# A depthwise convolution moved from VectorE, ScalarE and GpSimd to TensorE, with rows moved between partitions by DMA

## The chip, the cores and the metric

One core of one Trainium2 chip. The metric is the device time of one launch in microseconds (us), the median of the runs. The engines are PE (TensorE: matmuls, with PEld its weight loads), DVE (VectorE), ACT (ScalarE), POOL (GpSimd) and SP (SyncE, which here issues every DMA).

## What is computed

One block of a hybrid network over 512 tokens of 1024 channels, plus 256 context tokens, in float32: a modulated RMS norm, then two mixers on the same input (a Conformer convolution and a latent attention with 8 heads), merged by gates and one projection, then a SwiGLU feed-forward part and a final norm. The part that matters here is the convolution:

```python
def conformer_conv(conv_in, w_dw, b_dw, ln_g, ln_b, w_pw):
    a, g = jnp.split(conv_in, 2, axis=-1)
    u = a * jax.nn.sigmoid(g)
    u = lax.conv_general_dilated(
        u, w_dw[:, None, :], window_strides=(1,),
        padding=((CONV_WIDTH // 2, CONV_WIDTH // 2),),
        dimension_numbers=('NWC', 'WIO', 'NWC'),
        feature_group_count=D_CONV) + b_dw
    u = jax.nn.silu(layer_norm(u, ln_g, ln_b))
    return u @ w_pw
```

It is depthwise: every one of the 1024 channels has 31 taps of its own along the tokens. The layer norm behind it needs all channels, so nothing of the convolution is read before all eight of its tiles are done.

## The kernel before, in words

Activations lie transposed: a tile has 128 channels as partitions and the 512 tokens as columns. Every product of the block is made of three matmuls (`mm3`, L137 to L139): an operand is split into a high part that TensorE's float32r takes whole and the low rest (`split`, the high part by ACT at L104, the low by DVE at L105; for weights `split_w`, ACT L121 and DVE L125), and hi x hi, hi x lo and lo x hi are summed in PSUM. Weights come from HBM as tiles `wr` by SP (`load_w`).

After a prologue whose order is written out by hand (to about 140 us) comes the attention, where a scheduler orders each engine by a priority that grows along the program. The loop over the heads h runs, in this order: two quarters of `scores(h, qb)` (10 matmuls each at L468 and L469 into one of two PSUM buffers `ps_s`, then the maximum on DVE, the exponential and the scaling on ACT); half of `conv_steps(h + 2)`; the other two quarters; the rest of `conv_steps`; `prep(h + 1)`, which makes the next head's queries and keys; gates in heads 6 and 7 (`gate_mla`); and `attend(h)`: for each of six blocks of keys four transposes of the probabilities (L486), a split into `ph` and `pl`, and three matmuls with the values.

`conv_steps(i)` makes tile i of the convolution's input, `u`: 48 matmuls at L319, and the gate product at L333, in a tile with 15 columns of zeros at each side. `conv_taps(i, u)` is the depthwise convolution of this tile, 31 taps. For the tiles of `DVE_TILES`, 1, 4 and 7, all 31 taps are a chain on DVE (L344, L346), each adding a shifted copy of `u` times one weight per partition to an accumulator in PSUM. For the other five ACT scales the shifted copy (L351) and POOL adds it (L352). The taps are put in with a priority 3000 later than their place (`later(TAPS_LATER)`), so that other work goes first where it is ready. All engines run their instructions in order, once the scheduler has laid them down.

After the attention come the remaining gates, the layer norm of the convolution's tiles, the projections, and the feed-forward part, with PE as the engine that is hardly ever idle.

Of the kernel before, what the change touches and what calls it, by code (L numbers as in the profile page):

```python
# [18 lines left out]
P = 128  # L19
D = 1024  # L20
KD = D // P
S = 512
C = 256
H = 8
TAPS = 31
PAD = TAPS // 2
FF = 2816
KF = FF // P
EPS = 1e-6
TAPS_LATER = 3000  # L30
# [13 lines left out]
WK_AT = (1, 4)  # L44
MODS = (3, 3, 3)
MCOLS = (2, 4, 7)
DVE_TILES = (1, 4, 7)
PE_KC = (2, 2, 2, 2, 2, 2, 2, 2)
WARM = (34, 9, 3)
SCALE = (128 + 64) ** -0.5  # L50
# [1 line left out]
VEC = {}  # L52
_off = 0
for _n, _w in (("c", 8), ("cc", 8), ("b_mod", 48), ("g_mix", 8), ("g_ffn", 8), ("g_q", 3), ("g_kv", 2),
               ("b_dw", 8), ("ln_g", 8), ("ln_b", 8), ("g_final", 8), ("w_dw", 8 * TAPS)):
    VEC[_n] = (_off, _off + _w)
    _off += _w
NVEC = _off
# [3 lines left out]
def block_kernel(ctx: ExitStack, tc: tile.TileContext, I, out):  # L62
# [2 lines left out]

    cp = ctx.enter_context(tc.tile_pool(name="cp", bufs=1))
    wp = ctx.enter_context(tc.tile_pool(name="wp", bufs=3))
    ap = ctx.enter_context(tc.tile_pool(name="ap", bufs=60))
    tp = ctx.enter_context(tc.tile_pool(name="tp", bufs=3))
    sm = ctx.enter_context(tc.tile_pool(name="sm", bufs=4))  # L70
    bp = ctx.enter_context(tc.tile_pool(name="bp", bufs=4))
# [92 lines left out]
    bm1 = cp.tile([P, 16], F32, name="bm1")  # L164
    dve.tensor_scalar(out=bm1[:, 0:8], in0=v("b_mod", 8, 8), scalar1=1.0, scalar2=None, op0=ALU.add)
    dve.tensor_scalar(out=bm1[:, 8:16], in0=v("b_mod", 32, 8), scalar1=1.0, scalar2=None, op0=ALU.add)
    wdw = cp.tile([P, KD * TAPS], F32, name="wdw")
    dve.tensor_scalar(out=wdw, in0=v("w_dw"), scalar1=0.5, scalar2=None, op0=ALU.mult)
    modc = cp.tile([P, 32], F32, name="modc")

    def rstd_cols(ps, n, nb):
# [21 lines left out]
    def ps_x(n=512):  # L193
        return pp.tile([P, 512], F32, tag="x", name=nm("px"), bufs=4)[:, 0:n]
# [125 lines left out]
                yield  # L320

    def conv_steps(i, wg=None, wa=None):
        u = bp.tile([P, S + 2 * PAD], F32, tag="u", name=nm("u"), bufs=4)
        yield u
        ps = ps_x()
        yield from mm_steps(ps, wg or wtile(I["w_in"][3 + KD + i]), hx)
        sg = temp()
        act.activation(sg, ps, AF.Tanh, scale=0.5)
        ps = ps_x()
        yield from mm_steps(ps, wa or wtile(I["w_in"][3 + i]), hx)  # L330
        pool.memset(u[:, 0:PAD], 0.0)
        pool.memset(u[:, PAD + S:], 0.0)
        dve.scalar_tensor_tensor(out=u[:, PAD:PAD + S], in0=sg, scalar=1.0, in1=ps, op0=ALU.add, op1=ALU.mult)  # L333

    def conv_taps(i, u):
        a = slot()
        conv[i] = a
        acc = ps_x() if i in DVE_TILES else a
        for j in range(TAPS):
            wcol = wdw[:, i * TAPS + j:i * TAPS + j + 1]  # L340
            src = u[:, j:j + S]
            if i in DVE_TILES:
                if j == 0:
                    dve.tensor_scalar(out=acc, in0=src, scalar1=wcol, scalar2=v("b_dw", i), op0=ALU.mult, op1=ALU.add)  # L344
                else:
                    dve.scalar_tensor_tensor(out=a if j == TAPS - 1 else acc, in0=src, scalar=wcol, in1=acc, op0=ALU.mult, op1=ALU.add)  # L346
            elif j == 0:
                act.activation(a, src, AF.Identity, scale=wcol, bias=v("b_dw", i))
            else:
                t = bp.tile([P, S], F32, tag="tap", name=nm("tap"), bufs=3)  # L350
                act.activation(t, src, AF.Copy, scale=wcol)  # L351
                pool.tensor_tensor(out=a, in0=a, in1=t, op=ALU.add)  # L352

    def evac(ps, n=512):
        h, l = slot(F32R), slot(F32R)
# [121 lines left out]
        act.activation(p, p, AF.Copy, scale=r)  # L477
        return p

    def attend(h, ps_):  # L480
        g, e = h // 2, h % 2
        po = ps_x()
        for kb in range(6):
            pt = ps_x()
            for qb in range(4):
                pe.transpose(pt[:, qb * P:(qb + 1) * P], ps_[qb][:, kb * P:(kb + 1) * P], ident)  # L486
            ph, pl = pair()
            split(pt, ph, pl)
            vh, vl = vt[g][kb // 2]
            o = (kb % 2) * 256 + e * P  # L490
            mm3(po, vh[:, o:o + P], vl[:, o:o + P], ph, pl, kb == 0, kb == 5)
        a = slot()
        act.copy(a, po)
        o_t[h] = a

    def gate_w(i, after=None):
        raw = wp.tile([P, D], F32, tag="wr", name=nm("wr"))
# [19 lines left out]
    with tc.manual_schedule(engines={ET.PE, ET.DVE, ET.Activation, ET.Pool, ET.SP}):  # L517
# [230 lines left out]
        stack_q(1, terms)  # L748
        prep_kc(*wu, 768, 0, kx)
        prep_v(*wv, 0)  # L750
    with later(TAPS_LATER):
        conv_taps(0, u0)
        conv_taps(1, u1)

    for h in range(H):
        pr = [scores(h, qb) for qb in range(2)]
        if h < 6:
            it = conv_steps(h + 2)
            u = next(it)
            pump(it, 24)  # L760
        pr += [scores(h, qb) for qb in range(2, 4)]
        if h < 6:
            pump(it, 99)
            with later(TAPS_LATER):
                conv_taps(h + 2, u)
        if h + 1 < H:
            prep(h + 1)
        if h == 6:
            gate_mla(0, o_t[4])
        if h == 7:  # L770
            gate_mla(1, o_t[5])
            gate_mla(2, o_t[5])
        attend(h, pr)
    for i in range(3, KD):
        gate_mla(i, o_t[6])

# [1 line left out]
    if True:  # L778
# [73 lines left out]
                    dve.tensor_tensor(out=ssqs[q], in0=ssqs[q], in1=sq, op=ALU.add)  # L852

        for i in range(KD):
            t = slot() if i < 5 else bp.tile([P, S + 2 * PAD], F32, tag="u", name=nm("x2"), bufs=4)[:, 0:S]
            act.copy(t[:, 0:1], m1[0][:, 0:1])
            sp.dma_start(out=t, in_=I["xT"][:, i, :])
            x2.append(t)
# [310 lines left out]
```

## Time and profile before

| | |
|---|---|
| median of 3 runs | 1100.34 us (1097.81 to 1101.49) |
| the profiled execution | 1095.09 us |
| its span in the profile | 1093.3 us |
| mean granted clock of TensorE in it | 0.945 |
| PE busy | 972.0 us (89%) |
| DVE busy | 640.0 us (59%) |
| ACT busy | 525.4 us (48%) |
| POOL busy | 283.8 us (26%) |

Times are in us from the start of the span unless marked ns. An engine is busy while an instruction runs on it; register, branch, semaphore and DMA-issuing instructions don't count. [...] A name such as `px<-ph,stackr` means that the instruction writes `px` and reads `ph` and `stackr`; "idle before" is the time that the engine stood still just before an instruction, and the releaser is the instruction whose end it waited for. Matmuls are pipelined, so the time of one is longer than the step from one start to the next.

### The profile page before, as it was taken

To read this page: it belongs to the slowest core of one execution; us is meant where nothing else is said; L and a number is where in the kernel's file an instruction comes from. 1 tells how busy PE (TensorE), PEld (TensorE's weight loads), DVE (VectorE), ACT (ScalarE), POOL (GpSimd) and SP (SyncE) were. 2 spreads that over 40 slices of the span, in tenths; PEclk is the share of its full clock that TensorE was granted. 3 is DMA by queue.
4 is the path that set the end of the run, shared out by engine and by line. 5 is a ranking of instruction groups with operands and counts; after the bars stand their busy time and mean duration, and the time that the engine had idled before them with its cause. 6 is when DMAs were issued, how large, how long until landed. Compare 5 with 4: busy or idle time off the path is not lost.

```text
span 1093.3 us, 13176 instructions
## 1 busy us (share of the span) xinstructions
PE 972.0 (89%) x4772; PEld 812.0 (74%) x4772; DVE 640.0 (59%) x1052; ACT 525.4 (48%) x963; POOL 283.8 (26%) x237
## 2 busy tenths in 40 slices
PE   8789990988199962999999999999999999999996
PEld 8677880766187752777887888988888888888886
DVE  6997894465846568443589686483653333333333
ACT  4566686888168971554437223353333323332222
POOL 3766168998109991000000000020000000000000
PEclk9889995989599995999999999999999999999998
DMA  9801320011011000123363865133542223333312
GB/s 340 295 20 47 97 74 28 13 58 29 19 32 39 22 20 0 39 95 98 97 211 121 262 205 198 63 99 99 178 133 100 98 86 96 92 95 98 106 54 78
DMA packets 40721, 107.54 MB, mean 98 GB/s; under 512 B 4432, under 2 KB 6736, under 8 KB 40656
## 3 DMA queue, kind: packets, MB, share of 16 engines
q1 hardware_dynamic: 40656, 106.70, 30.3%
q8 instruction: 37, 0.61, 0.2%
q14 instruction: 28, 0.23, 0.1%
HBM read 104.59 MB, written 2.10 MB: 98 GB/s over the span
## 4 chain that ended last, share of the span: by engine, by line
PE 65%; DVE 13%; POOL 8%; ACT 8%; issue 5%; DMA 0%; POOLq 0%; SPq 0%; DVEq 0%; ACTq 0%
PE px L137 12%; PE px L138 11%; PE px L139 11%; POOL a L352 8%; PE ps L138 7%; PE ps L139 7%; PE ps L137 7%; DVE px L346 4%; DVE gm L263 2%; ACT tap L351 2%; PE ps L468 2%; DVE wl L125 2%; ACT p L477 1%; PE px L319 1%; ACT p L474 1%
## 5 line engine op out<-in xcount | busy, mean ns | idle before, releaser
L125 DVE TENSOR_TENSOR wl<-wr,wh 128x512 fp32r<-128x512 f32 (+1 forms) x264 | 197.2, 755 | 238.7 <-ACT wh L121 235.9
L121 ACT CAST wh<-wr 128x512 fp32r<-128x512 f32 (+2 forms) x274 | 164.5, 608 | 295.0 <-PE px L138 141.8
L137 PE MATMUL px<-a,wh 128*128 128x512 f32 (+1 forms) x607 | 224.2, 371 | 1.6 <-DVE t L417 1.0
L352 POOL TENSOR_TENSOR a<-a,tap 128x512 f32<-128x512 f32 x150 | 202.1, 1348 | 86.3 <-ACT tap L351 58.9
L138 PE MATMUL px<-a,wh 128*128 128x512 f32 (+1 forms) x607 | 223.1, 368 | 1.2 <-DVE a L722 1.1
L139 PE MATMUL px<-a,wl 128*128 128x512 f32 (+1 forms) x607 | 222.7, 367 | 0.0
L175 POOL TENSOR_TENSOR s<-s,mhalf 128x2 f32<-128x2 f32 (+1 forms) x10 | 9.3, 932 | 687.5 <-DVE s L173 687.5
L138 PE MATMUL ps<-a,wh 128*128 128x512 f32 (+1 forms) x376 | 141.6, 376 | 0.9 <-DVE a L921 0.8
L137 PE MATMUL ps<-a,wh 128*128 128x512 f32 (+1 forms) x376 | 141.5, 376 | 0.0
L139 PE MATMUL ps<-a,wl 128*128 128x512 f32 (+1 forms) x376 | 141.2, 375 | 0.0
L137 PEld LDWEIGHTS px<-a,wh 128*128 128x128 f32 x607 | 114.3, 188 | 22.1 <-ACT a L104 1.5
L138 PEld LDWEIGHTS px<-a,wh 128*128 128x128 f32 x607 | 114.4, 188 | 21.7 <-DVE a L722 2.0
L139 PEld LDWEIGHTS px<-a,wl 128*128 128x128 f32 x607 | 114.3, 188 | 18.9
L351 ACT ACTIVATE tap<-u,wdw 128x512 f32<-128x512 f32 x150 | 105.1, 722 | 33.8 <-POOL a L352 30.0
L138 PEld LDWEIGHTS ps<-a,wh 128*128 128x128 f32 x376 | 70.7, 188 | 14.3 <-DVE a L921 1.5
L319 PE MATMUL px<-a,wh 128*128 128x512 f32 x256 | 80.7, 393 | 0.0
L139 PEld LDWEIGHTS ps<-a,wl 128*128 128x128 f32 x376 | 70.8, 188 | 12.8
L137 PEld LDWEIGHTS ps<-a,wh 128*128 128x128 f32 x376 | 70.8, 188 | 12.6
L468 PE MATMUL ps<-a,a 128*128 128x512 f32 x160 | 60.1, 411 | 12.8 <-ACT a L104 12.8
L486 PE MATMUL px<-cst,p 128*128 128x128 f32 x192 | 30.7, 288 | 42.6 <-DVE a L346 42.2
L346 DVE SCALAR_TENSOR_TENSOR px<-u,wdw,px 128x512 f32<-128x512 f32 x87 | 65.6, 754 | 2.7
L486 PEld LDWEIGHTS px<-cst,p 128*128 128x128 f32 x192 | 25.2, 150 | 47.6 <-DVE a L346 42.6
(196 smaller groups left out, 1436.2 us busy)
## 6 DMA issues: line engine op xcount, KB each, us to landing
wr<-in_w_dram SPq DMA_DIRECT2D x60, 512.0 KB, 3.5
wr<-in_w_in_dram SPq DMA_DIRECT2D x35, 512.0 KB, 3.6
p<-in_w_mod_dram SPq DMA_DIRECT2D x64, 256.0 KB, 4.1
a<-in_w_mod_dram SPq DMA_DIRECT2D x32, 256.0 KB, 5.7
wr<-in_w_o_dram SPq DMA_DIRECT2D x8, 512.0 KB, 5.2
wr<-in_w_pw_dram SPq DMA_DIRECT2D x8, 512.0 KB, 5.6
wr<-in_w_out_dram SPq DMA_DIRECT2D x8, 512.0 KB, 3.7
a<-in_xT_dram SPq DMA_DIRECT2D x13, 256.0 KB, 5.6
```

Of the source, the lines that this page charges most:

```text
L121: act.copy(h, raw[:, i * WB:i * WB + h.shape[-1]])
L125: (eng or dve).tensor_tensor(out=l, in0=raw[:, i * WB:i * WB + h.shape[-1]], in1=h.bitcast(F32), op=ALU.subtract)
L137: pe.matmul(ps, lhsT=wh, rhs=ah, start=first, stop=False)
L138: pe.matmul(ps, lhsT=wh, rhs=al, start=False, stop=False)
L139: pe.matmul(ps, lhsT=wl, rhs=ah, start=False, stop=last)
L263: dve.scalar_tensor_tensor(out=gm[k], in0=slab(k, kc), scalar=sc[:, kc:kc + 1], in1=gm[k], op0=ALU.mult, op1=ALU.add)
L319: pe.matmul(ps, lhsT=l, rhs=r, start=k == 0 and i == 0, stop=k == n - 1 and i == 2)
L346: dve.scalar_tensor_tensor(out=a if j == TAPS - 1 else acc, in0=src, scalar=wcol, in1=acc, op0=ALU.mult, op1=ALU.add)
L351: act.activation(t, src, AF.Copy, scale=wcol)
L352: pool.tensor_tensor(out=a, in0=a, in1=t, op=ALU.add)
L468: pe.matmul(s[:, 0:512], lhsT=l[:, q0:q0 + P], rhs=rx_, start=i == 0, stop=i == 4)
L486: pe.transpose(pt[:, qb * P:(qb + 1) * P], ps_[qb][:, kb * P:(kb + 1) * P], ident)
```

## The change

The taps leave DVE, ACT and POOL. For a group of 32 channels, `tap_rows` has SP move the 32 rows of `u` (now its high and its low part side by side) four times from one place of SBUF to another, into the four quarters of the partitions of a tile `ur`, each copy 8 columns further on. A column of `ur` then holds 32 channels at four shifts. `tap_group` multiplies it by block matrices (`w_dwx`, 512 KB for a tile of 128 channels, made on the host): with `m` choosing one of two further shifts of 4 and the four quarters of the output `j` being shifts of 0 to 3, 4 x 2 x 4 = 32 taps, the last of them zero. That is two halves of 258 columns, each with two times three matmuls. ACT copies the sum to `e`, and SP moves each quarter of `e`, shifted by its `j`, to the rows of the 32 channels in one of four tiles `parts`. `tap_sum` adds the four on DVE. The moves of shifted rows stand in the program at the beginning of a head, the groups in `attend` after key blocks 1 to 4, the sum after the scores of the next head. The factor 0.5 of the gate goes from the weights to the copy `e`.

```diff
-    ap = ctx.enter_context(tc.tile_pool(name="ap", bufs=60))
+    ap = ctx.enter_context(tc.tile_pool(name="ap", bufs=58))
...
-    wdw = cp.tile([P, KD * TAPS], F32, name="wdw")
-    dve.tensor_scalar(out=wdw, in0=v("w_dw"), scalar1=0.5, scalar2=None, op0=ALU.mult)
...
     def conv_steps(i, wg=None, wa=None):
-        u = bp.tile([P, S + 2 * PAD], F32, tag="u", name=nm("u"), bufs=4)
+        u = bp.tile([P, 2, UPAD], F32R, tag="u", name=nm("u"), bufs=2)
...
-        dve.scalar_tensor_tensor(out=u[:, PAD:PAD + S], in0=sg, scalar=1.0, in1=ps, op0=ALU.add, op1=ALU.mult)
-
-    def conv_taps(i, u):
-        a = slot()
...
+        dve.scalar_tensor_tensor(out=sg, in0=sg, scalar=1.0, in1=ps, op0=ALU.add, op1=ALU.mult)
+        split(sg, u[:, 0, PAD:PAD + S], u[:, 1, PAD:PAD + S])
+
+    def tap_rows(u, g):
+        ur = bp.tile([P, 2, UW], F32R, tag="ur", name=nm("ur"), bufs=4)
+        for s_ in range(4):
+            sp.dma_start(out=ur[32 * s_:32 * s_ + 32].bitcast(F32), in_=u[32 * g:32 * g + 32, :, 8 * s_:8 * s_ + UW].bitcast(F32))
+        return ur
+
+    def tap_group(w, ur, g, parts):
+        ps = ps_s()
+        for q in range(2):
+            dst = ps[:, q * 512:q * 512 + HW]
+            for m in range(2):
+                o = (2 * g + m) * P
+                x = 4 * m + HW * q
+                mm3(dst, wc(w[0], o), wc(w[1], o), ur[:, 0, x:x + HW], ur[:, 1, x:x + HW], m == 0, m == 1)
+        e = bp.tile([P, 2 * HW], F32, tag="e", name=nm("e"), bufs=3)
+        act.activation(e.rearrange("p (q n) -> p q n", q=2), ps.rearrange("p (q n) -> p q n", q=2)[:, :, 0:HW], AF.Copy, scale=0.5)
+        for j in range(4):
+            sp.dma_start(out=parts[j][32 * g:32 * g + 32, :], in_=e[32 * j:32 * j + 32, j:j + S])
+
+    def tap_sum(i, parts):
+        a = parts[0]
         conv[i] = a
...
+        dve.scalar_tensor_tensor(out=a, in0=parts[1], scalar=v("b_dw", i), in1=a, op0=ALU.add, op1=ALU.add)
+        for t in parts[2:]:
+            dve.tensor_tensor(out=a, in0=a, in1=t, op=ALU.add)
...
-    def attend(h, ps_):
+    def attend(h, ps_, urs):
         g, e = h // 2, h % 2
         po = ps_x()
+        w = wtile(I["w_dwx"][h])
+        parts = [slot() for _ in range(4)]
...
+            if 1 <= kb <= 4:
+                tap_group(w, urs[kb - 1], kb - 1, parts)
...
+        return parts
...
-    with later(TAPS_LATER):
-        conv_taps(0, u0)
-        conv_taps(1, u1)
-
+    us = [u0, u1]
+    parts = None
     for h in range(H):
+        urs = [tap_rows(us[h], g) for g in range(4)]
         pr = [scores(h, qb) for qb in range(2)]
         if h < 6:
             it = conv_steps(h + 2)
-            u = next(it)
+            us.append(next(it))
             pump(it, 24)
         pr += [scores(h, qb) for qb in range(2, 4)]
         if h < 6:
             pump(it, 99)
-            with later(TAPS_LATER):
-                conv_taps(h + 2, u)
+        if parts:
+            tap_sum(h - 1, parts)
         if h + 1 < H:
             prep(h + 1)
...
-        attend(h, pr)
+        parts = attend(h, pr, urs)
+    tap_sum(7, parts)
```

What the scheduler makes of it on three engines, each row one instruction or several alike (the number behind a name is the buffer's):

DVE, before, around the taps of tile 4 (`u_2388` is that tile, `px_2503` the accumulator in PSUM, `a_2556` a part of head 3's query, which PE takes next):

```order
L333 SCALAR_TENSOR_TENSOR u_2388<-t_2462,px_2464 128x512
L125 TENSOR_TENSOR wl_2775<-wr_2770,wh_2773 128x512
L344 TENSOR_SCALAR px_2503<-u_2388,wdw,vec 128x512
L346 SCALAR_TENSOR_TENSOR px_2503<-u_2388,wdw,px_2503 128x512 x5
L125 TENSOR_TENSOR wl_2903<-wr_2899,wh_2901 128x512
L125 TENSOR_TENSOR wl_2904<-wr_2899,wh_2902 128x512
L346 SCALAR_TENSOR_TENSOR px_2503<-u_2388,wdw,px_2503 128x512 x24
L346 SCALAR_TENSOR_TENSOR a_2502<-u_2388,wdw,px_2503 128x512
L101 SCALAR_TENSOR_TENSOR a_2556<-px_2545,a_2555 128x512
```

All 31 taps of the tile stand ahead of the query's split; with the change these rows L344 and L346 are gone from DVE.

PE, now, in `attend(0)` (`px_1681` takes the transposes of a key block, `px_1623` gathers the head's output, `ps_1693` is the second group of taps):

```order
L495 MATMUL px_1681<-cst,p_1530 128x128
L138 MATMUL ps_1693<-ur_1409,wh_1626 128x258
L139 MATMUL ps_1693<-ur_1409,wh_1626 128x258
L140 MATMUL ps_1693<-ur_1409,wl_1628 128x258
L138 MATMUL ps_1693<-ur_1409,wh_1626 128x258
L139 MATMUL ps_1693<-ur_1409,wh_1626 128x258
L140 MATMUL ps_1693<-ur_1409,wl_1628 128x258
L138 MATMUL px_1623<-ph_1686,a_1382 128x512
L138 MATMUL ps_1693<-ur_1409,wh_1626 128x258
```

Before, the product of a key block stood right behind transposes; now tap matmuls are laid between the two.

DVE, now, at the scores of head 4 (`a_2985` to `a_2988` are the four `parts` of tile 3, the rows at L478 the maxima of the four quarters):

```order
L478 TENSOR_REDUCE s_3189<-ps_3178 128x1
L483 RECIPROCAL s_3175<-s_3173 128x1
L357 SCALAR_TENSOR_TENSOR a_2985<-a_2986,vec,a_2985 128x512
L483 RECIPROCAL s_3194<-s_3192 128x1
L359 TENSOR_TENSOR a_2985<-a_2985,a_2987 128x512
L359 TENSOR_TENSOR a_2985<-a_2985,a_2988 128x512
L478 TENSOR_REDUCE s_3244<-ps_3233 128x1
L478 TENSOR_REDUCE s_3263<-ps_3252 128x1
```

The three additions of partial sums, new here, stand between the maxima of the first two quarters and of the last two.

SP, now, from the last moves of head 6 (`e_4335` is its fourth group; `wr_4454` and `wr_4492` are the weights of the two gates of head 7):

```order
L352 DMA a_4203<-e_4335 32x512
L352 DMA a_4204<-e_4335 32x512
L338 DMA ur_4355<-u_3584 32x2x520 x4
L338 DMA ur_4360<-u_3584 32x2x520 x4
L338 DMA ur_4365<-u_3584 32x2x520 x4
L338 DMA ur_4370<-u_3584 32x2x520 x4
L512 DMA wr_4454<-in_w_in_dram 128x1024
L512 DMA wr_4492<-in_w_in_dram 128x1024
```

Before, the gates' loads (`wr_4188` and `wr_4226` there) followed on other weight loads with nothing between; now 20 moves stand ahead of the first of them.

## Rows read from the trace of the kernel before

**Rows 1.** Busy us by stretch: stretch, length, PE, PEld, DVE, ACT, POOL (instructions), PEclk, DMA share, GB/s
```profile
178.00:191.00 13.00, 1.69 (x6) 1.19 (x7) 1.19 (x2) 8.18 (x14) 11.00 (x14) 0.50 0.00 0
...
269.00:297.00 28.00, 0.64 (x3) 0.65 (x4) 25.14 (x34) 5.08 (x9) 8.38 (x8) 0.57 0.11 35
297.00:402.00 105.00, 101.52 (x511) 83.07 (x510) 59.13 (x84) 84.03 (x146) 68.71 (x51) 0.98 0.10 30
402.00:432.00 30.00, 1.46 (x7) 1.19 (x7) 26.35 (x34) 7.74 (x13) 12.66 (x10) 0.57 0.00 0
...
sum 317.00, PE 223.63 PEld 184.24 DVE 197.41 ACT 211.73 POOL 202.00; mean PE 31.95 PEld 26.32 DVE 28.20 ACT 30.25 POOL 28.86
```
**Rows 2.** Busy us by stretch, in the feed-forward part
```profile
900.00:1000.00 100.00, 100.00 (x443) 82.80 (x442) 36.03 (x56) 31.14 (x54) 0.00 (x0) 1.00 0.32 95
```
**Rows 3.** PE in order of time: start, us, what [idle before <-releaser]
```profile
177.87 0.47 PE L486 MATMUL px<-cst,p 128*128 128x128 f32 x1 [14.76 <-DVE a L346]
...
190.30 0.80 PE L468 MATMUL ps<-a,a 128*128 128x512 f32 x1 [11.31 <-ACT a L104]
...
296.36 0.48 PE L486 MATMUL px<-cst,p 128*128 128x128 f32 x1 [27.44 <-DVE a L346]
...
431.11 0.77 PE L432 MATMUL px<-ph,stackr 128*128 128x512 f32 x1 [28.54 <-DVE a L346]
```
**Rows 4.** Busy us by stretch, just after waits of PE
```profile
190.30:194.30 4.00, 4.00 (x13) 3.32 (x14) 1.73 (x4) 2.78 (x5) 3.77 (x4) 0.50 0.00 0
228.00:236.00 8.00, 5.56 (x26) 4.82 (x25) 6.81 (x8) 6.49 (x12) 7.76 (x8) 0.57 0.21 67
296.30:300.30 4.00, 3.94 (x12) 3.00 (x13) 2.22 (x5) 0.59 (x1) 0.00 (x0) 0.50 0.00 0
431.10:435.10 4.00, 3.99 (x15) 3.61 (x16) 2.09 (x4) 0.60 (x1) 0.00 (x0) 0.50 0.00 0
```
**Rows 5.** PE in order of time, the rotary chain of head 2
```profile
226.78 0.50 PE L432 MATMUL px<-ph,stackr 128*128 128x512 f32 x1 [1.19 <-ACT ph L104]
...
229.19 0.79 PE L432 MATMUL px<-pl,stackr 128*128 128x512 f32 x1 [0.95 <-DVE pl L105]
...
231.47 0.58 PE L372 MATMUL px<-wh,a 128*128 128x256 f32 x1 [1.49 <-DVE a L101]
```
**Rows 6.** PE in order of time, first and last of 36 matmuls with 256 columns
```profile
136.50 0.28 PE L372 MATMUL px<-wh,a 128*128 128x256 f32 x1
...
140.70 0.28 PE L374 MATMUL px<-wh,a 128*128 128x256 f32 x1
```
**Rows 7.** PE in order of time, two quarters of scores, then half a convolution's product
```profile
140.82 0.40 PE L468 MATMUL ps<-a,a 128*128 128x512 f32 x1
...
144.35 0.40 PE L319 MATMUL px<-a,wh 128*128 128x512 f32 x1
...
149.86 0.39 PE L468 MATMUL ps<-a,a 128*128 128x512 f32 x1
```
**Rows 8.** Groups by line, ACT (143 to 440 us) and DVE (143 to 460 us): busy, mean ns | idle before
```profile
L121 ACT CAST wh<-wr 128x512 fp32r<-128x512 f32 (+1 forms) x37 | 21.5, 586 | 2.7 <-PE px L319 2.7
L493 ACT COPY a<-px 128x512 f32<-128x512 f32 x5 | 2.9, 572 | 1.8 <-PE px L139 1.8
...
L125 DVE TENSOR_TENSOR wl<-wr,wh 128x512 fp32r<-128x512 f32 (+1 forms) x37 | 43.2, 1171 | 23.6 <-ACT wh L121 23.6
L105 DVE TENSOR_TENSOR pl<-px,ph 128x512 fp32r<-128x512 f32 x36 | 23.7, 686 | 22.7 <-ACT ph L104 22.3
```
**Rows 9.** SP's issues in order of time; and DMA issues: count, KB each, median us to landing
```profile
1.18 3.95 SPq L520 DMA_DIRECT2D a<-in_xT_dram  x8
5.17 3.01 SPq L240 DMA_DIRECT2D a<-in_w_mod_dram  x4
...
wr<-in_w_in_dram SPq DMA_DIRECT2D x35, 512.0 KB, 3.6
...
out_dram<-a SPq DMA_DIRECT2D x4, 128.0 KB, 2.5
```

More of the change, by code (lines that the diff above doesn't have):

```diff
@@ L29 @@
 EPS = 1e-6
-TAPS_LATER = 3000
 WB = 512
@@ L46 @@
 MCOLS = (2, 4, 7)
-DVE_TILES = (1, 4, 7)
+UPAD = 544
+UW = 520
+HW = 258
 PE_KC = (2, 2, 2, 2, 2, 2, 2, 2)
@@ L54 @@
 for _n, _w in (("c", 8), ("cc", 8), ("b_mod", 48), ("g_mix", 8), ("g_ffn", 8), ("g_q", 3), ("g_kv", 2),
-               ("b_dw", 8), ("ln_g", 8), ("ln_b", 8), ("g_final", 8), ("w_dw", 8 * TAPS)):
+               ("b_dw", 8), ("ln_g", 8), ("ln_b", 8), ("g_final", 8)):
     VEC[_n] = (_off, _off + _w)
@@ L330, in conv_steps @@
         yield from mm_steps(ps, wa or wtile(I["w_in"][3 + i]), hx)
-        pool.memset(u[:, 0:PAD], 0.0)
-        pool.memset(u[:, PAD + S:], 0.0)
-        dve.scalar_tensor_tensor(out=u[:, PAD:PAD + S], in0=sg, scalar=1.0, in1=ps, op0=ALU.add, op1=ALU.mult)
-    def conv_taps(i, u):
-        a = slot()
-        conv[i] = a
[L338 to L352, printed above, removed]
+        pool.memset(u[:, :, 0:PAD].bitcast(F32), 0.0)
@@ new lines, in conv_steps @@
+        pool.memset(u[:, :, PAD + S:].bitcast(F32), 0.0)
+        dve.scalar_tensor_tensor(out=sg, in0=sg, scalar=1.0, in1=ps, op0=ALU.add, op1=ALU.mult)
[17 more added lines that the diff above has]
+            sp.dma_start(out=parts[j][32 * g:32 * g + 32, :], in_=e[32 * j:32 * j + 32, j:j + S])
@@ L854, in block_kernel @@
         for i in range(KD):
-            t = slot() if i < 5 else bp.tile([P, S + 2 * PAD], F32, tag="u", name=nm("x2"), bufs=4)[:, 0:S]
+            t = slot() if i < 5 else bp.tile([P, 2 * UW], F32, tag="ur", name=nm("x2"), bufs=4)[:, 0:S]
             act.copy(t[:, 0:1], m1[0][:, 0:1])
@@ L1125, in _layout @@
             _cols(i["g_q"]), _cols(i["g_kv"]), _cols(i["b_dw"]), _cols(i["ln_g"]), _cols(i["ln_b"]),
-            _cols(i["g_final"]),
-            i["w_dw"][0].reshape(TAPS, KD, P).transpose(2, 1, 0).reshape(P, KD * TAPS)], axis=1),
+            _cols(i["g_final"])], axis=1),
+        "w_dwx": _tap_blocks(i["w_dw"][0]),
         "w_mod01": mod[:, :, 0:2].transpose(3, 1, 0, 2, 4).reshape(KD, P, KD, 256),
@@ L1140, in _layout, with _tap_blocks @@
     return {n: np.ascontiguousarray(x) for n, x in o.items()}
+def _tap_blocks(w):
+    pad = np.zeros((32, D), np.float32)
+    pad[:TAPS] = w
+    pad = pad.reshape(4, 2, 4, KD, 4, 32)
+    o = np.zeros((KD, 4, 32, 4, 2, 4, 32), np.float32)
+    for c in range(32):
+        o[:, :, c, :, :, :, c] = pad[..., c].transpose(3, 0, 4, 1, 2)
+    return o.reshape(KD, P, D)
 SHAPES = {
     "xT": (P, KD, S), "ctxT": (P, 4, 2 * C), "cst": (P, 1664), "vec": (P, NVEC),
-    "w_mod01": (KD, P, KD, 256), "w_mod25": (4, KD, P, D), "w_q": (KD, P, 768), "w_in": (35, P, D),
+    "w_dwx": (KD, P, D), "w_mod01": (KD, P, KD, 256), "w_mod25": (4, KD, P, D), "w_q": (KD, P, 768), "w_in": (35, P, D),
     "w_uq": (4, P, 1664), "w_uv": (4, P, 512), "w_o": (KD, P, D), "w_pw": (KD, P, D), "w_out": (KD, P, D),
```

## The prediction

> **What bounds the kernel now.** I read the busy table by stretches first. From 143 us, a few us into the eight attention heads, to 460 us PE is busy 223.6 of 317 us, and the idle part is not spread out: the stretch 297 to 402 us is busy 101.5 of 105, while 178:191, 269:297 and 402:432 are nearly empty [rows 1]. The reader is to see there that this is the one place where the kernel does not run at PE's pace; later PE is full, as the stretch 900:1000 shows [rows 2]. Next the order of PE's instructions with their idle time: four waits of 14.76, 11.31, 27.44 and 28.54 us, together 82.05 us [rows 3]. Three of them end with `DVE a L346`, the last of the 31 chained tap instructions that `conv_taps` puts on DVE for tiles 1, 4 and 7. PE does not read that tile. DVE runs in order, and behind the 31 taps stand the reductions and splits that PE does wait for (first order excerpt). The wait of 11.31 us ends with an ACT split, of the same jam. [...]
>
> **What goes.** The sum is made against the profiled execution, 1095.1 us with 1.8 us of it outside the span; the median of the runs, 1100.3, is 5.2 us above it.
> 1. The four waits: -82.05 us, as no engine carries a chain of taps any more.
> 2. The restarts at half clock: in the three windows of 4 us PE is busy 4.00, 3.94 and 3.99 us at 0.50 [rows 4]. At full clock half of that is enough: -6.0 us.
> 3. The waits in the rotary chain of head 2, 1.19, 0.95 and 1.49 us [rows 5], stand behind ACT and DVE work that is late because of taps; in 228:236 the clock is 0.57 with PE busy 5.56 us [rows 4], a loss of 5.56 x 0.43 = 2.4 us. Together -6.0 us. It is my choice to take all of it; nothing taken would be the other end.
>
> POOL loses 5 x 30 additions and ACT 5 x 31 scalings, those of the five tiles that DVE doesn't have. Off PE's path this is worth nothing by itself.
>
> **What comes.**
> 4. On PE 8 heads x 4 groups x 2 halves x 2 x 3 = 384 matmuls with 258 columns. No row has 258. With 256 columns 36 of them start between 136.50 and 140.70 us, a step of 0.120 us [rows 6]; two more columns make 0.121. With 512 columns it is 0.23: 24 of them, those of a convolution, start between 144.35 and 149.86 us [rows 7]. I take 0.121, since 258 is nearest to 256: 384 x 0.121 = +46.5 us, all on PE, which is then the bound. The other end is 0.23: +88 us. A matmul of more columns is not cheaper than one of 256, so nothing lies below 0.12. In the second order excerpt they stand between the transposes and the products of `attend`, so they also fill the short waits for the split there.
> 5. On ACT 32 copies `e` (about 0.57, as the copy of 512 from PSUM), six splits of `u` in this stretch (0.59) and 16 splits of the tap blocks (0.59) [rows 8]: 31 us. On DVE 24 additions of partial sums, 16 low parts of the blocks (1.17, beside POOL's work) and six of `u` [rows 8]: at most 54 us even at 1.17 each. Added to the 211.7 and 197.4 us of now [rows 1], taps not even taken off, this is 243 and 251 us in a stretch of about 279 (317 - 94 + 56). Both stay under PE: 0. If PE were faster than I think, DVE would be next.
> 6. DVE's wait for the moved partial sums (`tap_sum`, at the front of the third excerpt): behind it are the third and fourth quarter's maxima. The last move leaves 0.6 + 4 x 0.49 us after the last group of taps (the copy, then four issues, the step from item 7) and lands 2.5 us later, as 128 KB do [rows 9]: 5.1 us after the group. PE comes to the third quarter after two quarters of scores (3.53 us, 20 matmuls from 140.82 to 144.35 [rows 7]), 24 matmuls of a convolution (5.5) and the third quarter itself (1.8): 10.8 us. Covered: 0. In heads 6 and 7 no convolution stands there, but the sums stand later in DVE's order: 0.
> 7. SP gets 256 moves between partitions and eight loads of tap blocks. Eight issues in a row took 3.95 us, 0.49 each, four others 3.01 us, 0.75 each, while eight earlier transfers of 256 KB were still landing [rows 9]. The program hands out eight semaphores in turn, so a move also waits for the eighth before it: 2.5/8 = 0.31 us at the landing of 128 KB. I take 0.49. A head has 32 moves, 15.7 us, and PE needs about 279/8 = 35 us for a head. So the queue is not the bound; what counts is who stands behind the moves. In most heads the weights that PE needs next are loaded a head ahead. In head 7 they aren't: the weight of the gate that PE multiplies right after the scores stands behind four moves of partial sums and all 16 moves of shifted rows (fourth excerpt), and the rows' buffers come free only with the last group of head 6. From that group's end: 0.6 (copy) + 20 x 0.49 (moves) + 0.3 + 3.6 (landing of 512 KB [rows 9]) + 0.6 (split) = 14.9 us, against 2 x 3.53 = 7.1 us of scores (40 matmuls) that PE has meanwhile. A new wait of 7.8 us, and, as after the four waits of now [rows 4], 4 us at half clock after it, which cost 2: +9.8 us. If the weight came in time it would be 0; with the steps of 0.75 it is 15 (rival A).
> 8. Elsewhere: the smaller `vec` load and the dropped scaling of the taps, against two more splits in the part before 143 us, are under 1 us. One split in the feed-forward part moves in DVE's order, as two buffers are gone, beside a PE busy 100 of 100 us and DVE 36 [rows 2]: 0. All of PE's order after the attention is the same.
>
> Sum: 1095.1 - 82.05 - 6.0 - 6.0 + 46.5 + 9.8 = 1057.3, and on the scale of the runs 5.2 more. I say **1062 us**.
>
> [...] By the rows a move costs an issue slot of 0.49 us [rows 9]. [...] No run here shows moves of 32 partitions.
>
> **The rivals.**
> A. *Moves at 0.75 us each.* For it: the four issues at 0.75 [rows 9]. Head 7 then waits 0.6 + 20 x 0.75 + 4.5 - 7.1 = 13 us, 5.2 more. In heads 2 and 4 the weight of the next preparation stands behind 19 moves: 0.6 + 14.3 + 4.5 = 19.4 us, against 7.1 + 48 x 0.23 = 18.1 us of scores and convolution: 1.3 each. 1062 + 8 = 1070. Against it: those four issues had 2 MB landing before them, and here the DMA engines are a tenth busy [rows 1].
> B. *Everything short goes too.* Moves at 0.31, the step of the eight semaphores: head 7 waits 4.2 us and not 7.8, 3.6 less. And of PE's idle 93.4 us (317 less 223.6 [rows 1]) I have taken out only 82.05 and 3.63; the 7.7 that are left are mostly waits of `attend` and of scores for a split, between which tap matmuls would now stand. 1062 - 3.6 - 7.7 = 1051. Against it: some of these waits are in places with no tap group ahead of them.
> C. *The moves bound every head (slower).* With 32 moves at p and some 2 us of loads per head against 35 us of PE, SP sets the pace from p = 1.03 us on, and each 0.1 more costs 256 x 0.1 = 26 us. The gain of 38 is eaten at about p = 1.2, that is a landing of 9.6 us with eight in flight; at 1.3 it would be some 1062 + 70 = 1132. PE would then wait for `ur` ahead of the groups of every head. Against it: the longest issue step in the rows is 0.75, and 128 KB land in 2.5 us [rows 9]. For it: no transfer from SBUF to SBUF is in the trace at all, so neither number is of the thing itself.
> D. *258 columns cost as much as 512.* 384 x (0.23 - 0.121) = +42: 1104, no change. That the two columns over 256 could matter is all that speaks for it: no row has such a width.
>
> **How the numbers follow.** The forecast's own case (1055 to 1066) 0.50, A and other delays of its kind up to 1085 0.24, B (1046 to 1055) 0.14, D or a mix that ends within the old time 0.05, C 0.07. A measurement of this kernel can tell about 0.3% from no change, 3.3 us; of D's 0.05 I put 0.03 inside that and 0.02 on the fast side. So faster 0.90, same 0.03, slower 0.07. The range from 1046 to 1085 takes in B, the forecast and A, 0.88 in all, and leaves out C and D; each of the three has to be in it or more than 2 in 10 would be left out.
>
> **What would show it.** Right: PE without a wait of over 3 us between 143 us and the end of head 6, 384 matmuls at a step near 0.121, clock 1.0 there, and one wait of about 8 us before a gate's product in head 7 that ends with the split of its weight. The stretch then takes about 279 us where it took 317. Wrong: waits of PE for `ur` in many heads (C), a step well above 0.125 (D), moves issued every 0.7 us (A), DVE's waits in `tap_sum` followed by a wait of PE for `p`.

## The result and the profile after

The changed kernel takes 1062.34 us (median of 4 runs, 1060.80 to 1064.02) where the kernel before, run beside it, takes 1099.51: a ratio of 0.966, with a 95% interval from 0.964 to 0.969. The forecast was 1062, in a range from 1046 to 1085. The execution that was profiled took 1062.85 us, its span is 1061.1.

First, busy time by stretches of the changed kernel, the view of [rows 1] (stretch, length, busy us and instructions of PE, PEld, DVE, ACT and POOL, PEclk as the clock granted to TensorE in shares of full speed, DMA share, GB/s):

```profile
143.00:241.00 98.00, 97.81 (x546) 83.55 (x546) 51.79 (x85) 56.48 (x100) 0.37 (x4) 1.00 0.43 114
241.00:248.00 7.00, 4.93 (x20) 3.39 (x19) 3.63 (x7) 4.23 (x8) 0.00 (x0) 0.95 0.29 92
248.00:326.00 78.00, 77.80 (x436) 66.33 (x435) 39.47 (x64) 40.78 (x73) 0.37 (x4) 0.98 0.50 130
...
333.00:428.00 95.00, 94.43 (x555) 81.04 (x554) 47.52 (x78) 50.97 (x95) 0.19 (x2) 1.00 0.44 111
428.00:446.00 18.00, 7.28 (x29) 5.71 (x29) 8.05 (x14) 9.77 (x19) 0.00 (x0) 0.72 0.84 233
446.00:506.00 60.00, 59.97 (x295) 49.98 (x294) 24.11 (x39) 23.32 (x48) 0.00 (x0) 1.00 0.42 133
```

The empty stretches of [rows 1] are gone; PE is full but for two notches of 7 us and one of 18. These are the waits in them, PE in order of time, the view of [rows 3]:

```profile
245.59 0.50 PE L138 MATMUL px<-a,wh 128*128 128x512 f32 x1 [1.99 <-ACT wh L122]
...
330.39 0.50 PE L138 MATMUL px<-a,wh 128*128 128x512 f32 x1 [1.99 <-ACT wh L122]
...
441.66 0.80 PE L138 MATMUL px<-a,wh 128*128 128x512 f32 x1 [10.72 <-ACT wh L122]
```

All three end with a weight's split. SP's issues around the last one show why that split was late, as do the groups of DMA issues (count, KB each, median us to landing), beside [rows 9]:

```profile
423.45 3.12 SPq L352 DMA_DIRECT2D a<-e  x5
426.74 10.45 SPq L338 DMA_DIRECT2D ur<-u  x16
437.28 1.03 SPq L512 DMA_DIRECT2D wr<-in_w_in_dram  x2
```
```profile
ur<-u SPq DMA_DIRECT2D x128, 130.0 KB, 2.4
...
a<-e SPq DMA_DIRECT2D x128, 64.0 KB, 2.0
```

The gate's weight is issued at 437.28 behind 16 moves of rows that took 10.45 us, while PE ran out of scores at 430.94. In these bursts and in the median of all 256 a move takes a slot of 0.63 to 0.66 us on SP, those of 64 KB about as much as those of 130 KB.

In heads 2 and 4 it was not the load that was late. In head 2 it was issued at 237.42 and had landed at 240.62, 3 us before PE ran out of work at 243.60. DVE and ACT there, in order of time:

```profile
243.64 0.69 DVE L332 SCALAR_TENSOR_TENSOR t<-t,px 128x512 f32<-128x512 f32 x1 [3.29 <-PE px L318]
244.41 0.62 ACT L105 CAST u<-t 128x512 fp32r<-128x512 f32 x1 [2.60 <-issue]
244.93 0.61 ACT L122 CAST wh<-wr 128x512 fp32r<-128x512 f32 x1
```

In ACT's order the weight's split (L122) stands behind the high part of the convolution's `u` (L105), which needs the gate product (L332), which needs the convolution's last matmul. Head 4 has the same: the load had landed at 325.43, and PE ran out at 328.40.

To see where the time went I cut both profiled executions at two matmuls that both have: the first of the scores (140.82 us before, 144.86 after) and the layer norm's mean (539.11 and 506.41). The attention between them took 398.29 us and takes 361.55, 36.74 less. Worked out from PE's records in it, with half of PE's busy time at a granted clock of 0.50 counted as a loss, the last column being the kernel before without any taps, from the experiments:

| us in the attention | before | after | without taps |
|---|---|---|---|
| PE's waits of over 3 us | 82.05 | 10.72 | 0 |
| PE's shorter waits | 12.36 | 5.12 | 2.49 |
| lost at half clock | 10.08 | 3.52 | 0 |
| PE's work at full clock | 293.8 | 342.2 | 292.3 |
| sum | 398.3 | 361.6 | 294.8 |

Of the rest, the part before the attention is 4.0 us longer and the part behind it 0.5. How much of the 4 us is of the change is open. At half clock that part lost 9.95 us in the kernel before and 14.99 after, but 8.5 to 16.2 in the profiled executions of the experiments, in versions of either kernel (14.94 in one of the kernel before, 8.53 in one of the changed kernel). Its length was 140.8 to 143.9 us in the four executions of the kernel before and its versions, 142.5 to 145.6 in the seven of the changed kernel and its versions: the ranges overlap, and the means are 2.5 us apart.

### The profile page after: what moved, and what is told of

It is laid out like the page before. It is cut to its first block, busy times and chain, and to the rows that moved or that the text cites. A ratio compares the mean times of both kernels' runs of the same rounds, so it can differ in the third digit from the quotient of the medians.

```text
span 1061.1 us, 14040 instructions
## 1 busy us (share of the span) xinstructions
PE 1017.3 (96%) x5156; PEld 858.0 (81%) x5156; DVE 578.6 (55%) x1006; ACT 460.7 (43%) x864; POOL 81.7 (8%) x87
## 4 chain that ended last, share of the span: by engine, by line
PE 83%; DVE 6%; issue 3%; DMA 3%; ACT 2%; SPq 2%; POOL 0%; POOLq 0%; DVEq 0%; ACTq 0%
PE px L138 14%; PE px L139 13%; PE px L140 13%; PE ps L139 9%; PE ps L138 9%; PE ps L140 9%; PE px L318 6%; PE ps L475 3%; DVE gm L262 2%; DMA a<-in_w_mod_dram 2%; PE px L495 2%; PE ps L476 1%; SPq L338 1%; PE px L439 1%; DVE wl L126 1%
## 5 line engine op out<-in xcount | busy, mean ns | idle before, releaser
L126 DVE TENSOR_TENSOR wl<-wr,wh 128x512 fp32r<-128x512 f32 (+2 forms) x280 | 186.4, 677 | 253.9 <-ACT wh L122 247.7
L122 ACT CAST wh<-wr 128x512 fp32r<-128x512 f32 (+1 forms) x290 | 172.9, 610 | 320.0 <-PE px L139 142.4
L140 PE MATMUL px<-a,wl 128*128 128x512 f32 (+1 forms) x607 | 224.8, 371 | 0.1
L138 PEld LDWEIGHTS px<-a,wh 128*128 128x128 f32 x607 | 115.8, 191 | 37.1 <-ACT wh L122 15.9
L140 PE MATMUL ps<-a,wl 128*128 128x512 f32 (+1 forms) x376 | 141.2, 375 | 0.0
L139 PEld LDWEIGHTS px<-a,wh 128*128 128x128 f32 x607 | 115.9, 191 | 23.2 <-DVE a L734 2.5
L140 PEld LDWEIGHTS px<-a,wl 128*128 128x128 f32 x607 | 115.9, 191 | 20.4 <-DVE wl L126 1.2
L140 PEld LDWEIGHTS ps<-a,wl 128*128 128x128 f32 x376 | 70.8, 188 | 12.8
L318 PE MATMUL px<-a,wh 128*128 128x512 f32 x256 | 80.7, 393 | 0.0
L106 DVE TENSOR_TENSOR pl<-px,ph 128x512 fp32r<-128x512 f32 x48 | 32.9, 690 | 40.6 <-ACT ph L105 40.1
L318 PEld LDWEIGHTS px<-a,wh 128*128 128x128 f32 x256 | 47.1, 188 | 9.5
L212 DVE SCALAR_TENSOR_TENSOR a<-p,sc,a 128x512 f32<-128x512 f32 x56 | 40.6, 747 | 19.8 <-DMA p<-in_w_mod_dram 19.7
L478 DVE TENSOR_REDUCE s<-ps 128x1 f32<-128x768 f32 x32 | 30.6, 957 | 36.0 <-PE ps L476 36.0
L318 PE MATMUL px<-a,wl 128*128 128x512 f32 x128 | 50.2, 392 | 0.0
```

Source lines behind the costliest of these rows:

```text
L106: dve.tensor_tensor(out=lo, in0=src, in1=hi.bitcast(F32), op=ALU.subtract)
L122: act.copy(h, raw[:, i * WB:i * WB + h.shape[-1]])
L126: (eng or dve).tensor_tensor(out=l, in0=raw[:, i * WB:i * WB + h.shape[-1]], in1=h.bitcast(F32), op=ALU.subtract)
L212: dve.scalar_tensor_tensor(out=acc[e], in0=md, scalar=sc[:, kc:kc + 1], in1=acc[e], op0=ALU.mult, op1=ALU.add)
L318: pe.matmul(ps, lhsT=l, rhs=r, start=k == 0 and i == 0, stop=k == n - 1 and i == 2)
L478: dve.reduce_max(nmx, s[:, 0:768], axis=AX.X, negate=True)
```

## The experiments

**The queue: moves of rows on POOL.**

```diff
-            sp.dma_start(out=ur[32 * s_:32 * s_ + 32].bitcast(F32), in_=u[32 * g:32 * g + 32, :, 8 * s_:8 * s_ + UW].bitcast(F32))
+            pool.dma_start(out=ur[32 * s_:32 * s_ + 32].bitcast(F32), in_=u[32 * g:32 * g + 32, :, 8 * s_:8 * s_ + UW].bitcast(F32))
```

> The changed kernel with the 128 moves of shifted rows issued by POOL and no longer by SP. Theory 1 (weights stand behind the moves in SP's queue): the three waits of PE left in the attention, 10.72 us in head 7 and 1.99 us in heads 2 and 4, go, with the half clock behind them (about 3.5 us), since the loads are then issued a head ahead: 1062.3 - 18 = about 1044 us. Theory 2 (the wait belongs to the weights themselves, their transfer or their split): 1062 us, no change. Theory 3 (POOL issues a move more slowly than SP, over 2.2 us each, 16 to a head of 35 us): PE waits for ur in every head, slower than 1062.

It took 1044.83 us, a ratio of 0.951 [0.949, 0.954] to the kernel before. PE has no wait over 0.6 us left in the attention, and the clock there is 1.00; the attention takes 343.55 us. POOL's timeline shows what else changed, since nothing stands ahead of the moves there:

```profile
214.81 2.11 POOL L338 DMA_DIRECT2D ur<-u  x4 [28.59 <-issue]
217.79 2.11 POOL L338 DMA_DIRECT2D ur<-u  x4 [0.87 <-PE ps L140]
220.64 1.58 POOL L338 DMA_DIRECT2D ur<-u  x3 [0.75 <-PE ps L140]
```

Four moves go out as soon as a tap group has freed a buffer (releaser L140), beside the groups of the same head. On SP they had to stand behind the moves of partial sums of the last group, as a burst. Theory 1's time holds: the 18 us go when the rows leave SP's queue. For the 10.72 us it is by theory 1's way, as the gate's loads go out earlier. For the two waits of 1.99 us, whose weights had landed in time, it is another: in this version the scheduler laid the weight's split ahead of that of `u` in ACT's order.

```profile
240.78 0.61 ACT L122 CAST wh<-wr 128x512 fp32r<-128x512 f32 x1
...
243.47 0.62 ACT L105 CAST u<-t 128x512 fp32r<-128x512 f32 x1 [0.37 <-DVE t L332]
```

This version beats both kernels.

**The queue: moves of rows on ACT.** The same edit with `act` in place of `pool`.

> The changed kernel with the 128 moves of shifted rows issued by ACT, in place of SP. If an issue takes about 0.6 us of ACT's own time as it does SP's, 16 of them are 10 us of a head in which ACT has about 20 us of work in 35, in front of splits that PE needs. Theory 1 (what counts is who stands behind the moves): the waits behind SP's queue go (18 us), but PE gets waits for ACT's splits, in most heads some us: 1050 to 1090 us, slower than with POOL's queue. Theory 2 (any queue that is not SP's will do): 1044 us as with POOL.

1045.19 us, 0.953 [0.951, 0.955]: theory 2 by the time. ACT's timeline, here at the groups of head 1, shows the issue (ACTq) beside the work of the same engine:

```profile
220.01 0.60 ACT L350 ACTIVATE e<-ps 128x516 f32<-128x516 f32 x1 [1.33 <-PE ps L140]
220.68 0.59 ACT L105 CAST ph<-px 128x512 fp32r<-128x512 f32 x1
220.69 0.59 ACTq L338 DMA_DIRECT2D ur<-u  x1
222.65 0.60 ACT L350 ACTIVATE e<-ps 128x516 f32<-128x516 f32 x1 [1.38 <-PE ps L140]
```

The issue at 220.69 and the split at 220.68 run at the same time; an issue takes 0.59 us here too, but this one lies beside an instruction of ACT that had already started. Where many moves follow each other, ACT's next instruction stands behind them, as at the beginning of head 7:

```profile
414.99 7.94 ACTq L338 DMA_DIRECT2D ur<-u  x12
422.98 0.90 ACT L481 ACTIVATE p<-ps,s 128x768 f32<-128x768 f32 x1 [7.41 <-DMA ur<-u]
```

ACT's exponentials had seven such waits, 47.0 us in sum. So my charge against ACT was right about ACT and wrong about PE, which had other work ready for most of that time: it waited 3.76 us in head 7, for the exponential above, and twice about 0.9 us. The attention took 344.98 us, 1.4 more than with POOL's queue.

**No moves at all.**

```diff
-        for s_ in range(4):
-            sp.dma_start(out=ur[32 * s_:32 * s_ + 32].bitcast(F32), in_=u[32 * g:32 * g + 32, :, 8 * s_:8 * s_ + UW].bitcast(F32))
+        pool.memset(ur.bitcast(F32), 0.5)
...
-        for j in range(4):
-            sp.dma_start(out=parts[j][32 * g:32 * g + 32, :], in_=e[32 * j:32 * j + 32, j:j + S])
+        pool.tensor_copy(parts[g], e[:, 0:S])
```

> Leaves out all 256 moves between partitions: the tiles of shifted rows are filled with a constant by POOL, and the partial sums are copied in their own partitions by POOL, so the convolution's values are not computed; the tap matmuls, the copies and the additions stay. Theory 1: only the three waits behind the moves go, about 18 us: 1044 us, as with the moves on another queue. [...]

1043.92 us, 0.951 [0.948, 0.954], as with POOL's queue (1044.83). The 256 transfers themselves, 25 MB beside a PE that is full, cost nothing that these runs can tell.

**Moves cut in two.** Each move of 32 partitions becomes two of 16, those of partial sums as shown and those of rows in the same way.

```diff
-            sp.dma_start(out=parts[j][32 * g:32 * g + 32, :], in_=e[32 * j:32 * j + 32, j:j + S])
+            for p in (0, 16):
+                sp.dma_start(out=parts[j][32 * g + p:32 * g + p + 16, :], in_=e[32 * j + p:32 * j + p + 16, j:j + S])
```

> The changed kernel with every move between partitions cut in two of 16 partitions: 512 moves with half the bytes each. Theory 1 (an issue takes SP 0.66 us whatever it moves): 64 issues are 42 us of a head, and with the weights' loads 44, where PE has about 40: SP sets the pace, PE waits in most heads, + 30 us, about 1090 us, and still more in head 7 (its weight stands behind 8 + 31 moves). Theory 2 (the step goes with the bytes or the partitions): 0.33 us each, no change, 1062 us.

1185.13 us, 1.080 [1.077, 1.082], slower than the kernel before. The slot is theory 1's: SP's issues at head 2 show 32 moves of half the bytes in 20.58 us, 0.64 each. The size isn't: + 123 us, not + 30.

```profile
248.55 20.58 SPq L339 DMA_DIRECT2D ur<-u  x32
269.17 1.06 SPq L110 DMA_DIRECT2D wr<-in_w_in_dram  x2
```

And PE in order of time:

```profile
273.98 0.80 PE L318 MATMUL px<-a,wh 128*128 128x512 f32 x1 [28.93 <-ACT wh L122]
...
390.35 0.80 PE L318 MATMUL px<-a,wh 128*128 128x512 f32 x1 [29.02 <-ACT wh L122]
...
506.17 0.80 PE L138 MATMUL px<-a,wh 128*128 128x512 f32 x1 [27.09 <-ACT wh L122]
...
589.47 0.80 PE L138 MATMUL px<-a,wh 128*128 128x512 f32 x1 [21.74 <-ACT wh L122]
```

I had reckoned with a rate, so many slots in a head against so much of PE's work. But the burst behind the last group stands as a whole ahead of the weights that PE takes next, and these four waits, 106.8 us, are, as I read them, bursts less what PE still had to do. SP was issuing for 304 of the attention's 483.6 us. Here even the convolution's weights (L318) come too late.

**The gate's weights of head 7 first.**

```diff
     for h in range(H):
+        if h == 7:
+            gw = [gate_w(19 + KD + i, o_t[5]) for i in (1, 2)]
         urs = [tap_rows(us[h], g) for g in range(4)]
...
-            gate_mla(1, o_t[5])
-            gate_mla(2, o_t[5])
+            gate_mla(1, w=gw[0])
+            gate_mla(2, w=gw[1])
```

> The changed kernel with the two gate weights of head 7 loaded ahead of head 7's 16 moves of shifted rows, everything else as it was. Theory 1: the first weight is issued 16 x 0.66 = 10.5 us earlier, the wait of 10.72 us shrinks to under 1.5 us and the half clock behind it (1.8 us) goes: about 1050 to 1051 us. The waits of 1.99 us in heads 2 and 4 stay. Theory 2 (transfer or split): 1062 us. A trap: the moves are now two issues later, which nobody should feel, as PE has two gates' products (11 us) before it needs the rows.

A miss: 1062.20 us, 0.967 [0.964, 0.969], what the changed kernel has. The weight is issued at 425.45 and lands at 429.34; counted from the first scores it is issued 10.9 us earlier than in the changed kernel. Yet PE waits 4.23 us for its split, then 0.72, then 2.40 in `attend`. ACT in order of time:

```profile
429.16 0.89 ACT L481 ACTIVATE p<-ps,s 128x768 f32<-128x768 f32 x1
...
430.75 0.90 ACT L481 ACTIVATE p<-ps,s 128x768 f32<-128x768 f32 x1 [0.62 <-DVE s L478]
431.55 0.19 ACT L481 ACTIVATION_READ_ACCUMULATOR p<-ps,s 128x1 f32 x1
431.64 1.75 ACT L484 ACTIVATE p<-p,s 128x768 f32<-128x768 f32 x2
433.29 2.17 ACT L122 CAST wh<-wr 128x512 fp32r<-128x512 f32 x4
```

The split stands behind the softmax of the last two quarters, which PE has just made. The wait of 2.40 us ends with a copy `e`, ahead of which ACT stood 2.68 us for the load of the next gate's weight; that was issued at 454.90, though the moves had ended at 438.08. The clock fell to 0.50 twice in head 7, not once. In sum the attention took 360.30 us, 1.2 less than in the changed kernel. With the moves on POOL's queue the loads go out earlier still, and no such wait is left.

**Every tap matmul twice.**

```diff
-        for q in range(2):
+        for q in (0, 1, 0, 1):
```

> The changed kernel with every matmul of the taps made twice (768 in place of 384, the second time from the start, so the sums are the same). Theory 1 (PE is the bound, 258 columns cost 0.121 to 0.126 us): + 46.5 to 48.4 us, 1107 to 1111 us. Rival (258 columns cost as much as 512, 0.23 us, and the first 384 were partly hidden in waits): + 88, 1150 us. Rival (the taps hide in the waits of the attention for its splits): + 30 or less, under 1092 us.

1106.41 us, 1.008 [1.006, 1.011] to the kernel before. The attention's full-clock work on PE grows from 342.2 to 388.0 us, 45.8 for 384 matmuls: 0.119 each. It is theory 1, a little below its figure of 1107; the waits in heads 2, 4 and 7 became 2.1 us shorter in sum. 258 columns cost what 256 do (0.120).

**The kernel before, with taps left out.** In three kernels 30 of 31 taps are left out: for the three tiles on DVE, for the five on ACT and POOL, for all. In the first and the last the accumulator in PSUM goes as well.

```diff
-        acc = ps_x() if i in DVE_TILES else a
-        for j in range(TAPS):
+        acc = a
+        for j in range(1 if i in DVE_TILES else TAPS):
```
```diff
-        for j in range(TAPS):
+        for j in range(TAPS if i in DVE_TILES else 1):
```
```diff
-        acc = ps_x() if i in DVE_TILES else a
-        for j in range(TAPS):
+        acc = a
+        for j in range(1):
```

> The kernel before, with 30 of the 31 taps left out for tiles 1, 4 and 7, those of the chain on DVE; the five tiles on ACT and POOL keep theirs. Theory 1 (DVE's chain holds what PE waits for): the four waits, 82.05 us, and the half clock behind three of them, 6 us, go: 1099 - 88 = about 1011 us. Theory 2 (the wait of 11.31 us, which ended with ACT, belongs to ACT's and POOL's taps): that one stays, with its 2 us of half clock: 1024 us. Theory 3 (DVE's chain only covers another jam, of ACT and POOL): over 1050 us.

> The kernel before, with 30 of the 31 taps left out for the five tiles on ACT and POOL; tiles 1, 4 and 7 keep their chain on DVE. It closes the square: all taps 1097, none 994, without DVE's 1045. Theory 1 (each chain holds PE at its own places, the sum is additive): 994 + 52 = 1046 us, with the waits of 27.44 and 28.54 us there and none near 163 to 190 us. Theory 2 (both chains hold the early waits, 14.76 and 11.31 us, so that either alone is enough): those stay too, 994 + 82 + 6 = about 1080 us.

> The kernel before, with 30 of the 31 taps left out for all eight tiles. Theory 1: beside the kernel without DVE's chain only the short waits of the rotary chain and of the splits go, up to 12 us with their half clock: about 1000 us. The changed kernel with its moves off SP's queue stood at 1044.8: its 384 matmuls at 0.121, 46.5 us, would put the same program without any taps at 998 us, so the two floors should agree within 3 us. If this is well below 998, the changed kernel still pays somewhere else; at 1011 or above, ACT's and POOL's taps cost nothing in the kernel before.

| taps | us | ratio to before, 95% interval |
|---|---|---|
| all (the kernel before) | 1097 to 1098 | |
| none on DVE | 1044.83 | 0.953 [0.951, 0.955] |
| none on ACT and POOL | 1055.24 | 0.962 [0.960, 0.964] |
| none | 994.34 | 0.906 [0.905, 0.908] |

Without DVE's taps I expected 1011 or 1024 and got 1045. PE in order of time, in that kernel:

```profile
171.32 0.80 PE L137 MATMUL px<-ph,a 128*128 128x512 f32 x1 [6.99 <-DVE pl L105]
...
187.94 0.47 PE L486 MATMUL px<-cst,p 128*128 128x128 f32 x1 [14.97 <-DVE a L101]
...
231.90 0.58 PE L372 MATMUL px<-wh,a 128*128 128x256 f32 x1 [4.67 <-DVE a L101]
```

The waits of 27.44 and 28.54 us are gone, but of the first two, 26.07 us [rows 3], 21.96 stay. ACT in the second of them (the rows left out are alike):

```profile
173.18 0.72 ACT L351 ACTIVATE tap<-u,wdw 128x512 f32<-128x512 f32 x1 [0.63 <-POOL a L352]
174.52 0.72 ACT L351 ACTIVATE tap<-u,wdw 128x512 f32<-128x512 f32 x1 [0.62 <-POOL a L352]
...
185.26 0.72 ACT L351 ACTIVATE tap<-u,wdw 128x512 f32<-128x512 f32 x1 [0.62 <-POOL a L352]
...
186.59 0.57 ACT L100 ACTIVATE a<-px 128x512 fp32r<-128x512 f32 x1
```

ACT starts a scaling every 1.34 us and not every 0.72: each needs one of three `tap` buffers, which POOL's additions free. From 171.8 to 185.9 us ACT does nothing else, and the split of the query (L100) stands behind it. So ACT was tied to POOL's pace, and PE to ACT. Without ACT's and POOL's taps, on the other hand, DVE's three chains alone hold PE for 10.93, 22.88 and 22.59 us:

```profile
174.37 0.48 PE L486 MATMUL px<-cst,p 128*128 128x128 f32 x1 [10.93 <-DVE a L346]
...
266.80 0.47 PE L486 MATMUL px<-cst,p 128*128 128x128 f32 x1 [22.88 <-DVE a L346]
...
390.57 0.77 PE L432 MATMUL px<-ph,stackr 128*128 128x512 f32 x1 [22.59 <-DVE a L346]
```

Against the kernel without any taps, ACT's and POOL's alone cost 50 us (1044.83 - 994.34) and DVE's alone 61 (1055.24 - 994.34), all together 103 to 104. That is nearly a sum, 7 to 9 us short of it, and lies between my two theories: both kinds jam the stretch from 163 to 190 us. Without any taps the attention takes 294.81 us, with PE busy for 292.32 at full clock:

```profile
143.93:438.74 294.81, 292.32 (x1493) 240.23 (x1492) 145.67 (x243) 160.56 (x293) 0.89 (x8) 1.00 0.19 58
```

The changed kernel with its moves on POOL's queue is 50 us above that, in the same view:

```profile
143.98:487.53 343.55, 342.18 (x1876) 290.61 (x1875) 175.80 (x287) 186.09 (x342) 60.05 (x122) 1.00 0.49 130
```

So what the taps cost in it is PE's work and, within a us or two, nothing else: 49.9 us for the first 384 tap matmuls (0.130 each, where the second 384 cost 0.119). What the 3 to 4 us between the two are was not looked into further.

## Why the prediction was right, point by point

The total was right, and both of its halves were about 10 us too small. By the experiment without taps, what the change removes from the attention is 398.3 - 294.8 = 103.5 us (I had 94), and what it adds is 361.6 - 294.8 = 66.8 (I had 56.3). The two misses cancelled, which is luck.

1. *The four waits, -82.05.* They all went. But the reason was half right: I gave all four to DVE's chain, because three rows named it as the releaser. The releaser is only the last of those that were late. For the first two, 26 us, ACT at POOL's pace was late as well, and would have held PE for 22 us alone. Nor does PE's restart wait for the reductions and splits behind the taps. DVE at the end of the third wait, in the kernel before:

```profile
295.55 0.75 DVE L346 SCALAR_TENSOR_TENSOR a<-u,wdw,px 128x512 f32<-128x512 f32 x1
296.22 0.69 DVE L101 SCALAR_TENSOR_TENSOR a<-px,a 128x512 fp32r<-128x512 f32 x1
```

PE's transposes start at 296.36 [rows 3], 0.06 us after the chain's end, while the query's split (L101) still runs. They read nothing that DVE writes; they write a `px`, of which there are four buffers in PSUM (`ps_x`), and the chain's accumulator held one. So that buffer is most likely what they waited for. The scores that need the split stand right behind them in PE's order, so that here it came to nearly the same. How much the buffer alone would have cost is not shown, since the runs that leave out DVE's taps leave out the accumulator too.
2. and 3. *Half clock, and the rotary chain, -6 and -6.* Too small, the main part of the miss on this side: without taps the short waits fall by 9.9 us (I took 3.6) and the loss at half clock by 10.1 (I took 8.4). This is where the sentence failed that ACT's and POOL's work, off PE's path, is worth nothing: the rotary chain's waits grew to 2.74, 0.95 and 4.67 us where only DVE's taps were out. That the remaining short waits go too was rival B, and without moves in the way it was the truer picture.
4. *384 matmuls at 0.121, +46.5.* Measured: 0.119 by doubling them, 0.126 to 0.130 by adding them. Rival D is out. That they also fill the waits of `attend` is hardly shown: the short waits fell from 12.36 to 5.12 us, but without any taps, with nothing to fill them, they are 2.49, and with the moves on POOL's queue 1.4. So filling can account for about 1 us.
5. *ACT and DVE under PE.* Right: in the attention's 361.55 us ACT is busy 189.0 and DVE 177.3.
6. *`tap_sum` covered.* Right: no wait of PE for probabilities behind it over 0.4 us.
7. *SP, +9.8.* The mechanism and the place were right: a wait in head 7 that ends with the gate's split, behind four moves of sums and 16 of rows. The size was not: the slot was 0.657 us, between my 0.49 and the other end, 0.75. Twenty slots more expensive by 0.167 make 3.3 us, and the wait was 10.72 and not 7.8. The waits in heads 2 and 4, 1.99 us each, look like those of 1.3 that I had only in rival A. But by A's own sum this slot gives none there (0.6 + 19 x 0.657 + 4.5 = 17.6 us against 18.1), and the weights had landed in time; what I had wrong is ACT's order, with the split of `u` ahead of the weight's. So A came true in 2.9 of its 8 us, and that the other 4.0 agree in size is luck. That the wait in head 7 would be 0 if the weight came in time was wrong for the same kind of reason: with the gate's weights first, 4.23 us of it stayed. I also divided wrongly: 143 to 460 us is not eight heads. A head of the changed kernel takes 32 to 44 us, so that rival C's point lay higher than the 1.03 us I gave for it. And cutting the moves in two showed that C works by another way than a rate: by the burst ahead of the next weights, while SP was issuing for 63% of the attention.
8. *The rest, 0.* Right within 0.5 us behind the attention. The 4 us ahead of it, where I had taken under 1, are in part the clock there, which differs from one execution to the next (8.5 to 16.2 us lost at half clock); the rest is open. They are most of the 5.5 us by which my sum for the profiled execution was too low (1057.3 against 1062.85), although the attention was foretold within 1 us. The step from that execution to the median, + 5.2, then made up for it: the changed kernel's profiled execution lies at its median and not 5 us below. So the last 5 us of the agreement are luck.

## What to carry to other kernels

A releaser names the last that was late, not the only one (of 26.07 us, 21.96 stayed without DVE's taps): before an entire wait is written to its account, ask which other in-order engine is jammed in the same stretch, and remove one chain at a time to see. The small DMAs here were paid by the slot in their queue and not by the byte (0.63 to 0.66 us from 32 to 130 KB), and what they cost is the burst that stands ahead of the next load that somebody waits for: 128 moves given to an engine with nothing to do saved 17.5 us of the 1062, while twice as many of half the size cost 123. Where a wait ends with a load's split, look first whether the load was late at all: in heads 2 and 4 it had landed 3 us early, and an earlier load helps only as far as the engine that splits has nothing ahead of it (issued 10.9 us earlier in head 7, it left 4.23 us of the wait).

## What the runs showed of the hardware that I had not expected

A move between partitions mostly took SP 0.63 to 0.66 us a slot with 32, 64, 65 and 130 KB alike, and landed in the median 2.0 to 2.4 us after its issue (3.7 us for the sums while POOL issued the rows). ACT issues one in 0.59 us beside an instruction of its own that has already started, but its next instruction stands behind a burst (7.41 us behind 12 moves). POOL issues one in 0.53 us, with a longer landing (a median of 4.3 us for 130 KB, where SP and ACT had 2.4 and 2.5), for which PE had no wait over 0.6 us.
